# A residual block with three-pass matmuls: late gate sigmoids, an output-weight load split between gate loads, and two broadcast rows on another queue

## The chip, the cores and the metric

The kernel runs on one core of a Trainium2 chip. The metric is the device time of one execution in microseconds (us). The time before is the median of three runs. One more execution was profiled; every duration below comes from that one.

## What is computed

One layer of a streaming encoder: 1024 tokens, width 1024, all in float32. The parts that matter here:

```
proj = h @ w_in                       # q, k, v, forget logits, g_b, g_c, hc, gate_conv, gate_attn
ya = g_b * conv3(g_c * hc)            # branch a, 512 wide
yb = softmax(q k / 8 + c_q - c_k) v   # branch b, 8 heads of 64; c = running sum of log-sigmoids
m  = sigmoid(gate_conv) * (ya @ w_branch[0]) + sigmoid(gate_attn) * (yb @ w_branch[1])
x  = x + rmsnorm(m @ w_out)
x  = x + rmsnorm(swiglu(rmsnorm(x)))
```

The order in which sums are formed is free; the gates, the two branch products and the sum `m` are what the change works on.

## The kernel before, in words

**Arithmetic.** Each float32 matmul is done as three float32r passes: an operand is split into a high half (ScalarE copies it, `split`, line 132) and a low half (VectorE subtracts), and `mm3` (line 137) issues high-high, high-low and low-high. On top of that the large products use a Strassen-like scheme: seven block products whose names (A11, A12, A22, S1 to S4 for the weight side, B11, B21, B22, T1 to T4 for the other) appear all over the code. The trace puts every instruction on line 77, since a wrapper records them, so groups are told apart by tile names.

**Stages.** Projection (`strassen` per pair of weight columns, `jobs` 0 to 18, loop index `ij`), the last of these beside the first steps of attention (`last_pair`, line 915), attention with branch a's products filled in (`pba`), then branch b, then `w_out` (tiles `p`, `q`, `b`), the norms, the feed-forward part.

**Order.** In most stages a scheduler may reorder an engine's instructions; `strict[0]` names the engines on which program order is kept. In branch b it is SyncE and TensorE first, then VectorE and ScalarE too (lines 1546 to 1596). SyncE issues almost all loads, GpSimd most stores. Each of them waits in order: a DMA whose buffer isn't free holds back everything that stands behind it on that queue.

**Branch b.** The products of w_branch[1] and yb come in three groups. The first products A11 and S1 fill eight PSUM banks, `pbanks` and `vbanks` (`pbp`, `pbv` in the trace). The first loop over u = 0 to 3 (line 1569) does S2 into `pbanks[u]`, S4 into `vbanks[u]`, S3 into `pbanks[u]`, 18 matmuls a turn. Between S2 and S3 ScalarE copies `pbanks[u]` to `u_s[u]` (tile `temps`), and S3 can't start before that copy. VectorE adds, then `merge` (line 1513) multiplies by a gate and adds the result into `um`. The second loop (line 1588) does A22 and A12, 12 matmuls a turn, with its own merges. After it `first` (line 1650) starts `w_out` with operands that `first_ops` (line 1462) splits from `um`, and `sums` forms the others.

**Gates.** Blocks 0 to 6 of gate_attn lie in DRAM (`sg_dram`) as sigmoids. Block 7 lies there raw, since its projection runs beside attention. `gate` (line 1496) loads a 256 KB half block and, for block 7, issues its sigmoid on ScalarE at once. Half n1 of blocks 0 to 3 is loaded ahead of the first loop into the four buffers of `sg`; blocks 4 to 7 reuse these as merges free them (`early`). For half n2, blocks 7, 6, 1 and 0 go into buffers `raw` and `sx`, the other four into `sg` again (`late`).

**w_out's first block.** `load_wo(B11, u)` on line 1562 loads the four quarters of tile `x0`, 512 KB each, from `wo_dram`, within the loop of S1.

**Attention's first rows.** `cb_of(j, e)` (line 746) broadcasts the row of c for one head to 128 partitions (tile `cb`, two buffers, 512 KB). The two buffers are at first `bh` and `bl`, from which `wb_load` (line 994) stores the split w_branch to `wb_dram` on GpSimd's queue, the last time in job 13. The first two rows are asked for in job 15 (line 1081). They are first used by `mask_of(0, 7)` in `last_pair`.

Of the kernel before, what the change touches and what calls it, by code (L numbers as in the profile page):

```python
# [12 lines left out]
AF = mybir.ActivationFunctionType  # L13
# [4 lines left out]
P = 128  # L18
S = 1024
D = 1024  # L20
KT = D // P
# [21 lines left out]
B11, B21, B22, T1, T2, T3, T4 = range(7)  # L43
# [4 lines left out]
def block_kernel(  # L48
# [20 lines left out]
    class InOrder:  # L69
# [15 lines left out]
    nc = SimpleNamespace(  # L85
        **{e: InOrder(e) for e in engines}
    )
# [28 lines left out]
    def mul(o, a, b):  # L116
        nc.vector.tensor_tensor(o, a, b, op=ALU.mult)
# [32 lines left out]
    c_dram = dpool.tile([H, S], F32, name="c_dram")  # L150
# [21 lines left out]
    ones = cpool.tile([P, P], F32, name="ones")  # L172
    nc.vector.memset(ones, 1.0)
    mask = cpool.tile([P, P], F32, name="mask")
    def bcast_row(row, p, **kw):
        g = p.tile([P, row.shape[-1]], F32, **kw)
        nc.sync.dma_start(g, row.partition_broadcast(P))
        return g

    def st_tile(name, w=1):  # L180
# [363 lines left out]
    def raw_t():  # L544
        return wtile("raw", 3)

    def hi_t():
        return wtile("hi", 4, F32R)

    def lo_t():  # L550
        return wtile("lo", 3, F32R)

    def s4_t():
        return wtile("s4", 1, F32, (P, 4, P))

    def s4h_t():
        return wtile("s4h", 2, F32R, (P, 4, P))

    def s4l_t():
        return wtile("s4l", 2, F32R, (P, 4, P))  # L560
# [129 lines left out]
    def wcols(c0):  # L690
        return win[:, c0 : c0 + P]
# [54 lines left out]
    def cb_of(j, e, again=False):  # L746

        key = j, e, again
        if key not in cbs:
            p = t1 if j % 2 and not again else t0_  # L750
            cbs[key] = bcast_row(c_dram[2 * j + e], p, tag="cb", name="cb", bufs=2)
        return cbs[key]

    cbs, qks, stacks, vs_, rsums = {}, {}, {}, {}, {}
# [288 lines left out]
    for ij, (kind, j, _, _) in enumerate(jobs):  # L1043
        work = side.pop(ij, [])

        def mid():
            for cut, _ in work:
                pinned(cut, "vector", "scalar")

        if ij == 2:  # L1050
            logf_pre = forget_sums()
        if ij == 4:
            cs_ = forget_store(*logf_pre)
        if ij == 5:
            forget_turn(cs_)
        if ij < 2:
            if ij == 0:
                r1 = raw_t()
                nc.sync.dma_start(r1, kmaj(wcols(jobs[1][2])))
                t0_.tile([P, S], F32, tag="p", name="room", bufs=2)  # L1060
                h1, l1 = (
                    kblk(t0_.tile([P, S], F32R, tag="cb", name=n, bufs=2)) for n in ("h1", "l1")
                )
                split(h1, l1, r1)
                heads = [prep_first(None, t) for t in ((r0, h0, l0), (r1, h1, l1))]
                for _ in range(2):
                    bank(psm, "spare")
                strict[0] = ("tensor", "scalar")
                firsts = strassen_firsts([w for w, _ in heads], h1b, psm, pp)
                strict[0] = ()  # L1070
            (w, r1), (c11, p1) = heads[ij], firsts[ij]
            w = {**w, **prep_rest(wcols(jobs[ij][3]), r1)}
            if ij == 1:
                pairs.q.append(pairs.prep(*pairs.srcs.popleft()))
            _, c12, c21, c22 = strassen(w, h1b, psm, pp, p1, mid)
        elif ij < len(jobs) - 1:
            if ij == 12:
                k_load(0)
                q_load(0)
            w = pairs.get()  # L1080
            if ij == 15:
                cb_of(0, 0)
                cb_of(0, 1)
            c11, c12, c21, c22 = strassen(w, h1b, psm, pp, None, mid)
        else:
            w = pairs.get()
            psm_close()
            strict[0] = engines
            pss, pss_close = pool("pss", space=PSUM)
            c11, c12, c21, c22 = last_pair(w)  # L1090
        if kind == "qk":
            so = pp.tile([P, NC], F32, tag="so", name="so")
            copy(so, c11)
            for r, c, t in ((0, n1, so), (0, n2, c12), (1, n1, c21), (1, n2, c22)):
                nc.gpsimd.dma_start(qk_dram[j][r, :, c], t)
        elif kind == "z":
            zt = z_tile("zt")
            mul(zt[:, n1], c21, c11)
            mul(zt[:, n2], c12, c22)
            zts[j] = zt  # L1100
        elif kind == "gb":
            for m, parts in ((j, (c11, c12)), (j + 1, (c21, c22))):
                zt = zts.pop(m)
                for n in range(2):
                    o = n * NC
                    ot = pp.tile([P, NC], F32, tag="so", name="ot")
                    nc.vector.tensor_scalar(
                        ot, zt[:, o : o + NC], cw[:, 2, m : m + 1], None, op0=ALU.mult
                    )
                    for t in (1, 0):  # L1110
                        back = 2 - t
                        skip = 0 if n else back
                        nc.vector.scalar_tensor_tensor(
                            ot[:, skip:], zt[:, o + skip - back : o + NC - back],
                            cw[:, t, m : m + 1], ot[:, skip:],
                            op0=ALU.mult, op1=ALU.add,
                        )
                    yt = ot if parts[n] is c11 else parts[n]
                    mul(yt, ot, parts[n])
                    nc.gpsimd.dma_start(ya_dram[m][:, o : o + NC], yt)  # L1120
        else:
            so = c11
            strict[0] = ()
            if ij < len(jobs) - 1:
                so = pp.tile([P, NC], F32, tag="so", name="so")
                nc.scalar.activation(so, c11, AF.Sigmoid)
                for t in (c12, c21, c22):
                    nc.scalar.activation(t, t, AF.Sigmoid)
            for r, c, t in ((0, n1, so), (0, n2, c12), (1, n1, c21), (1, n2, c22)):
                nc.gpsimd.dma_start(sg_dram[j][r, :, c], t)  # L1130
        for _, store in work:
            pinned(store, "scalar")
        if ij < len(jobs) - 2:
            side[ij + 1].append(wo_load(ij))
        if ij + 1 in WB_AT:
            side[ij + 1].append(wb_load(WB_AT.index(ij + 1)))
# [314 lines left out]
    def load_wo(o, k):  # L1451
        nc.sync.dma_start(f32(wo[o][:, :, k, :]), wo_dram[o, k])
# [9 lines left out]
    def first_ops(i, th, tl):  # L1462
        a = slice(2 * i * P, (2 * i + 1) * P)
        if i:
            split(th, tl, um[:, :, a])
            firsts[i] = dict(A11=(th[:, LO], tl[:, LO]), A12=(th[:, UP], tl[:, UP]))
        else:
            firsts[i] = {}
            for o, src, h, l in zip(("A11", "A12"), blocks(i), th, tl):
                split(h, l, src)  # L1470
                firsts[i][o] = h, l
# [8 lines left out]
    def sums(i, t):  # L1480

        a11, a12, a21, a22 = blocks(i)
        s3[i] = t
        minus(i, t, a11, a21)
        minus(i, a21, a21, a22, ALU.add)
        minus(i, a11, a21, a11)
        minus(i, a12, a12, a11)
# [8 lines left out]
    def gate(d, ns, sg=None):  # L1496
        sg = sg_tile() if sg is None else sg
        nc.sync.dma_start(sg, sg_dram[d][1, :, ns])
        if d == KT - 1:
            nc.scalar.activation(sg, sg, AF.Sigmoid)  # L1500
        return sg

    def prod_b(ps, o, u, b, first):
# [7 lines left out]
            )  # L1511

    def merge(d, ns, t, c, sg):
        mul(t, c, sg)
        add(um[:, d, ns], um[:, d, ns], t)

# [42 lines left out]
    for u in range(4):  # L1559
        prod_b(vbanks[u], S1, u, T1, True)  # L1560
        copy(v_s[u], vbanks[u])
        load_wo(B11, u)
    load_wbr(A22)
    late = [
        x for t in (wtile("raw", 3), wtile("sx", 1)) for x in kept_halves(flat(t))
# [3 lines left out]
    for u in range(4):  # L1569
# [9 lines left out]
        merge(2 * u + 1, n1, v_s[u], v_s[u], sg1)  # L1579
        if u < 2:  # L1580
            early += [gate(2 * u + 4 + x, n1) for x in range(2)]
    first_ops(0, [s4h_t(), s4h_t()], [s4l_t(), s4l_t()])
    sums(0, s4_t())
    first_ops(1, hi_t(), lo_t())
    late |= {u: [gate(2 * u + 1 - x, n2) for x in range(2)] for u in (1, 2)}
    for u in range(4):
        load_wo(B21, u)
    for u in range(4):
        prod_b(pbanks[u], A22, u, T4, False)
        copy(v_s[u], pbanks[u])  # L1590
        prod_b(vbanks[u], A12, u, B21, False)
        copy(u_s[u], vbanks[u])
        for x, t in enumerate((v_s[u], u_s[u])):
            sg = late[u][x]
            merge(2 * u + 1 - x, n2, sg, t, sg)
    strict[0] = ("sync",)
    for n, o in ((3, T1), (2, T2)):
        wo[o] = x_tile(n)
# [306 lines left out]
    for f in range(NF):  # L1905
# [15 lines left out]
        for g, u, ns in ((g1, u1_, n1), (g2, u2, n2)):  # L1921
            sg = sgs[:, ns]
# [160 lines left out]
    sums = {n: wide(f"sum_{n}") for n in ("c11", "c12", "c22", "c21", "both", "rest", "neg")}  # L2083
# [107 lines left out]
```

## Time and profile before

| | |
|---|---|
| median of three runs (range) | 1333.67 us (1333.49 to 1334.63) |
| the profiled execution | 1333.1 us |
| its span, first to last instruction | 1331.3 us |
| mean granted TensorE clock | 0.993 |
| TensorE busy | 1305.8 us, 98% of the span |
| VectorE, ScalarE, GpSimd busy | 984.7, 572.4, 153.9 us |
| HBM traffic | 176 GB/s over the span |

TensorE is busy nearly always, so what matters is where it is not, and where its clock is down. The list of waits says for whom an engine waited, in total, how often and how long at most. The timeline gives start, duration, engine, operation, and in brackets the idle time before an instruction with what ended it. Matmuls of 512 columns overlap: they are 0.39 us each but start closer together.

### The profile page before, as it was taken

The numbers are of one execution on the slowest core, as the hardware profiler recorded it, in microseconds if no ns is written. First come the engines' busy times: TensorE is split into PE (matmuls) and PEld (weight loads), VectorE is DVE, ScalarE is ACT, GpSimd is POOL, SyncE is SP. The second block draws the span as 40 slices with busy tenths as digits, with TensorE's granted clock in tenths as the row PEclk, the third lists the DMA queues.
The fourth block names the chain that finished last, engine by engine and source line by source line (L and its number), as shares of the span: only waits on it lengthen the run. The fifth ranks groups of instructions, "written<-read, shape, count | busy, mean of one in ns | idle before, by whom it ended". The sixth has DMA issues, their size and how long they took to land.

```text
span 1331.3 us, 18049 instructions
## 1 busy us (share of the span) xinstructions
PE 1305.8 (98%) x6686; PEld 1087.1 (82%) x6686; DVE 984.7 (74%) x1525; ACT 572.4 (43%) x910; POOL 153.9 (12%) x287
## 2 busy tenths in 40 slices
PE   9999999999999999959999999999999999999997
PEld 8988888888787888848888888888888888888886
DVE  6975978876566867639699688997767776676685
ACT  6642432244345866515577432322322233443452
POOL 0011100021112221001012112121011101000000
PEclk9999999999999999979999999999999999999999
DMA  6337755677855444558466555563233328875541
GB/s 221 114 113 219 211 156 144 185 242 205 226 154 179 159 144 159 197 190 311 179 221 200 180 165 183 168 195 103 73 119 103 119 91 285 316 257 190 158 166 64
DMA packets 207240, 235.13 MB, mean 177 GB/s; under 512 B 12064, under 2 KB 150368, under 8 KB 207152
## 3 DMA queue, kind: packets, MB, share of 16 engines
q1 hardware_dynamic: 159424, 157.13, 37.7%
q0 software_dynamic: 18544, 62.17, 12.7%
q10 hardware_dynamic: 29184, 14.68, 4.4%
q8 instruction: 52, 0.85, 0.3%
q14 instruction: 36, 0.29, 0.1%
HBM read 161.79 MB, written 72.16 MB: 176 GB/s over the span
## 4 chain that ended last, share of the span: by engine, by line
PE 73%; issue 17%; DMA 3%; POOL 2%; DVE 2%; ACT 1%; SPq 0%; DVEq 0%; POOLq 0%; ACTq 0%
PE b L77 36%; PE pd L77 16%; PE pba L77 3%; PE pv L77 3%; PE tps L77 3%; PE po L77 3%; PE p L77 2%; PE sp L77 2%; PE pbp L77 2%; PE ma L77 1%; DMA raw<-sg_dram 1%; PE q L77 1%; PE tp L77 1%; POOL wb_dram L77 1%; DMA wb_dram<-bl 1%
## 5 line engine op out<-in xcount | busy, mean ns | idle before, releaser
L77 PE MATMUL b<-x,hi 128*128 128x512 f32 x1088 | 335.4, 389 | 0.0
L77 PEld LDWEIGHTS b<-x,hi 128*128 128x128 f32 x1088 | 204.1, 188 | 42.4
L77 PE MATMUL b<-x,lo 128*128 128x512 f32 x544 | 211.7, 389 | 0.0
L77 DVE TENSOR_TENSOR c<-c,b 128x512 f32<-128x512 f32 x193 | 131.5, 682 | 47.0 <-PE b L77 38.6
L77 DVE TENSOR_TENSOR lo<-raw,hi 128x1024 fp32r<-128x1024 f32 x90 | 108.4, 1204 | 71.2 <-PE b L77 61.1
L77 ACT ACTIVATE hi<-raw 128x1024 fp32r<-128x1024 f32 (+1 forms) x96 | 97.4, 1017 | 94.0 <-PE b L77 46.7
L77 PEld LDWEIGHTS b<-x,lo 128*128 128x128 f32 x544 | 102.1, 188 | 21.2
L77 ACT ACTIVATE hi<-sx 128x1024 fp32r<-128x1024 f32 (+1 forms) x42 | 43.8, 1043 | 136.8 <-PE b L77 128.8
L77 ACT ACTIVATE sgf<-c 128x512 f32<-128x512 f32 x31 | 19.6, 633 | 131.9 <-DVE c L77 112.8
L77 DVE TENSOR_TENSOR lo<-sx,hi 128x1024 fp32r<-128x1024 f32 (+1 forms) x42 | 50.3, 1198 | 28.8 <-PE b L77 26.1
L77 DVE TENSOR_TENSOR sx<-raw 128x512 f32<-128x512 f32 x78 | 53.6, 687 | 19.7 <-DMA raw<-in_w_in_dram 10.7
L77 PE MATMUL pd<-hi,lo 128*128 128x512 f32 x160 | 62.3, 389 | 0.0
L77 PE MATMUL pd<-hi 128*128 128x512 f32 x160 | 61.9, 390 | 0.0
L77 PE MATMUL pd<-ghi 128*128 128x512 f32 x148 | 57.7, 390 | 0.0
L77 PE MATMUL pd<-glo,ghi 128*128 128x512 f32 x148 | 57.6, 389 | 0.0
L77 PE MATMUL pd<-ghi,glo 128*128 128x512 f32 x148 | 57.6, 389 | 0.0
L77 PE MATMUL b<-hT12h,lo 128*128 128x512 f32 x136 | 53.0, 390 | 0.0
L77 PE MATMUL b<-hT12h,hi 128*128 128x512 f32 x136 | 52.9, 389 | 0.0
L77 PE MATMUL b<-hT34h,lo 128*128 128x512 f32 x136 | 52.9, 389 | 0.0
L77 PE MATMUL b<-hT34h,hi 128*128 128x512 f32 x136 | 52.9, 389 | 0.0
L77 PE MATMUL b<-hT34l,hi 128*128 128x512 f32 x136 | 52.9, 389 | 0.0
L77 PE MATMUL b<-hT12l,hi 128*128 128x512 f32 x136 | 52.9, 389 | 0.0
(462 smaller groups left out, 3065.1 us busy)
## 6 DMA issues: line engine op xcount, KB each, us to landing
raw<-in_w_gate_up_dram SPq DMA_DIRECT2D x55, 512.0 KB, 3.9
raw<-in_w_in_dram SPq DMA_DIRECT2D x35, 512.0 KB, 5.9
x<-wo_dram SPq DMA_DIRECT2D x28, 512.0 KB, 7.8
a_dramS<-um POOLq DMA_DIRECT2D x44, 256.0 KB, 3.0
a_dramA<-um POOLq DMA_DIRECT2D x33, 256.0 KB, 2.7
wo_dram<-h ACTq DMA_DIRECT2D x16, 448.0 KB, 4.3
wo_dram<-l ACTq DMA_DIRECT2D x16, 448.0 KB, 4.8
sg<-sg_dram SPq DMA_DIRECT2D x28, 256.0 KB, 2.7
```

The source lines that it names most:

```text
L77: ins = getattr(self.engine, name)(*args, **kw)
```

## The change

Three edits. First, the sigmoid of a gate of block 7 moves from `gate` (at the load) into `merge` (at the use). Second, the four loads of `x0` leave the loop of S1 and go in pairs behind the gate loads of the first two turns of the first loop, and the block `first_ops(0)`, `sums(0)`, `first_ops(1)` moves from between the two loops to behind the first turn of the second one. Third, the first two broadcast rows are issued on GpSimd's queue, and in job 14 instead of 15; later rows stay on SyncE.

```diff
-    def bcast_row(row, p, **kw):
+    def bcast_row(row, p, by=None, **kw):
         g = p.tile([P, row.shape[-1]], F32, **kw)
-        nc.sync.dma_start(g, row.partition_broadcast(P))
+        (by or nc.sync).dma_start(g, row.partition_broadcast(P))
...
-            cbs[key] = bcast_row(c_dram[2 * j + e], p, tag="cb", name="cb", bufs=2)
+            by = nc.sync if j else nc.gpsimd
+            cbs[key] = bcast_row(c_dram[2 * j + e], p, by, tag="cb", name="cb", bufs=2)
...
-            if ij == 15:
+            if ij == 14:
                 cb_of(0, 0)
                 cb_of(0, 1)
...
         nc.sync.dma_start(sg, sg_dram[d][1, :, ns])
-        if d == KT - 1:
-            nc.scalar.activation(sg, sg, AF.Sigmoid)
         return sg
...
     def merge(d, ns, t, c, sg):
+        if d == KT - 1:
+            nc.scalar.activation(sg, sg, AF.Sigmoid)
         mul(t, c, sg)
...
         copy(v_s[u], vbanks[u])
-        load_wo(B11, u)
...
             early += [gate(2 * u + 4 + x, n1) for x in range(2)]
-    first_ops(0, [s4h_t(), s4h_t()], [s4l_t(), s4l_t()])
-    sums(0, s4_t())
-    first_ops(1, hi_t(), lo_t())
+            for k in range(2):
+                load_wo(B11, 2 * u + k)
...
             merge(2 * u + 1 - x, n2, sg, t, sg)
+        if u == 0:
+            first_ops(0, [s4h_t(), s4h_t()], [s4l_t(), s4l_t()])
+            sums(0, s4_t())
+            first_ops(1, hi_t(), lo_t())
```

The place on ScalarE where the sigmoids stood, before: `raw_5813` is block 7's half n2, `sg_5878` its half n1; `temps<-pbp` are the copies between S2 and S3.

```order
L77 ACTIVATE temps_5652<-pbv_5776 128x512
L77 ACTIVATE raw_5813<-raw_5813 128x512
L77 ACTIVATE temps_5652<-pbp_5709 128x512
L77 ACTIVATE pbv_5773<-p_s_5653 128x512
L77 ACTIVATE temps_5652<-pbp_5710 128x512
L77 ACTIVATE pbv_5774<-p_s_5653 128x512
L77 ACTIVATE sg_5878<-sg_5878 128x512
L77 ACTIVATE temps_5652<-pbp_5711 128x512
L77 ACTIVATE pbv_5775<-p_s_5654 128x512
```

The same engine now, from the third turn of the first loop on (`sg_5875` is the same half n1, the last `temps<-pbp_5709` belongs to the second loop):

```order
L77 ACTIVATE temps_5652<-pbp_5711 128x512
L77 ACTIVATE pbv_5775<-p_s_5654 128x512
L77 ACTIVATE temps_5652<-pbp_5712 128x512
L77 ACTIVATE pbv_5776<-p_s_5654 128x512
L77 ACTIVATE sg_5875<-sg_5875 128x512
L77 ACTIVATE temps_5652<-pbp_5709 128x512
L77 ACTIVATE temps_5652<-pbv_5773 128x512
L77 ACTIVATE s4h_5962<-um_3816 128x512
```

No sigmoid stands ahead of a copy of the first loop any more: half n1's follows the last of them, and half n2's the last copy of the second loop. The split of `um` for `first_ops(0)` (`s4h`) now follows the second loop's first two copies.

SyncE's loads in branch b, as the difference (`raw<-wb_dram` are A12's weights, the `hi` and `wbl` behind them A22's; then gates):

```order
 L77 DMA lo<-wb_dram 128x1024
 L77 DMA raw<-wb_dram 128x1024 x2
-L77 DMA x_5650<-wo_dram 128x2x512 x4
 L77 DMA hi<-wb_dram 128x1024
 L77 DMA wbl<-wb_dram 128x1024
...
 L77 DMA sg<-sg_dram_138 128x512
 L77 DMA sg<-sg_dram_139 128x512
+L77 DMA x_5650<-wo_dram 128x2x512 x2
 L77 DMA sg<-sg_dram_140 128x512
 L77 DMA sg<-sg_dram_141 128x512
+L77 DMA x_5650<-wo_dram 128x2x512 x2
```

The 2 MB of `x0` no longer stand ahead of A22's weights and the gates of blocks 7, 6, 1 and 0; they stand behind the gates of blocks 4 and 5, and 6 and 7.

GpSimd's queue around job 14, as the difference (`sg_dram_137` and `sg_dram_138` are stores of jobs' gates):

```order
 L77 DMA sg_dram_137<-c_3088 128x512
 L77 DMA wb_dram<-bl 128x2x512
+L77 DMA cb<-c_dram 128x1024
 L77 DMA sg_dram_137<-c_3072 128x512
+L77 DMA cb<-c_dram 128x1024
 L77 DMA sg_dram_138<-so 128x512
```

The two rows now stand behind the stores that free their buffers and ahead of two gate stores. On SyncE they stood between two weight loads (`raw<-in_w_in_dram`) of one job, which now follow each other.

## The prediction

> **What bounds the kernel now.** I read the page first. TensorE is busy for nearly the whole span, so a gain must come out of its gaps:
>
> ```profile
> PE 1305.8 (98%) x6686; PEld 1087.1 (82%) x6686; DVE 984.7 (74%) x1525; ACT 572.4 (43%) x910; POOL 153.9 (12%) x287
> ```
>
> Then TensorE's list of waits, of which two rows lie where the change works:
>
> ```profile
> PE pbp L77 <- ACT temps L77: 14.5, 2, 11.0
> ...
> PE b L77 <- ACT c L77: 0.7, 1, 0.7
> ```
>
> The first row is branch b's first loop, the second a gate job of the projection. TensorE's timeline shows where the long waits lie, and where the loops begin and end (564.30 is the first S2, 599.38 the first A22, 610.26 w_out's first matmul):
>
> ```profile
> 564.30 0.39 PE L77 MATMUL pbp<-yh,hi 128*128 128x512 f32 x1
> ...
> 566.80 0.39 PE L77 MATMUL pbv<-yh,lo 128*128 128x512 f32 x1
> 578.21 0.80 PE L77 MATMUL pbp<-yh,hi 128*128 128x512 f32 x1 [11.02 <-ACT temps L77]
> ...
> 592.20 0.50 PE L77 MATMUL pbp<-yh,hi 128*128 128x512 f32 x1 [3.44 <-ACT temps L77]
> ...
> 599.38 0.39 PE L77 MATMUL pbp<-yh,hi 128*128 128x512 f32 x1
> ...
> 610.26 0.62 PE L77 MATMUL p<-x,s4h 128*128 128x512 f32 x2
> ```
>
> ScalarE's timeline shows that the copies were not slow. They stood, in program order, behind a sigmoid whose gate had not landed:
>
> ```profile
> 577.04 0.63 ACT L77 ACTIVATE raw<-raw 128x512 f32<-128x512 f32 x1 [11.94 <-DMA raw<-sg_dram]
> 577.57 0.58 ACT L77 ACTIVATE temps<-pbp 128x512 f32<-128x512 f32 x1
> ...
> 591.03 0.63 ACT L77 ACTIVATE sg<-sg 128x512 f32<-128x512 f32 x1 [4.93 <-DMA sg<-sg_dram]
> 591.57 0.58 ACT L77 ACTIVATE temps<-pbp 128x512 f32<-128x512 f32 x1
> ```
>
> The waits cost clock too. Right after the long one the windows view gives a granted clock of 0.58 (third column from the end):
>
> ```profile
> 576.00:584.00 8.00, 5.79 (x16) 4.65 (x17) 4.14 (x6) 2.32 (x4) 0.00 (x0) 0.58 0.33 116
> ```
>
> **Branch b, first loop.** The second loop is undisturbed: 48 matmuls from 599.38 to 610.26, 10.88 us, 0.2267 us each. At that pace the 72 matmuls of the first loop take 16.32 us; they took 599.38 - 564.30 = 35.08. The excess is 18.76 us: waits of 11.02 and 3.44, and 4.30 of slow clock. If no sigmoid stands before a copy, the first copy can run when S2 ends, about 565.9, takes 0.58, and is done before S4 ends at 567.2. So the wait goes and S3 follows S4. Nothing is added: the two sigmoids, 0.63 each, go where ScalarE is idle most of the time.
>
> What is late next? The weights first. S3's low half is the later one, and A22's stands behind `x0`:
>
> ```profile
> 559.24 0.38 SPq L77 DMA_DIRECT2D lo<-wb_dram  x1
> ...
> 560.68 3.15 SPq L77 DMA_DIRECT2D x<-wo_dram  x4
> ...
> 564.65 0.43 SPq L77 DMA_DIRECT2D wbl<-wb_dram  x1
> 566.08 1.55 SPq L77 DMA_DIRECT2D raw<-sg_dram  x2
> ```
>
> The issue views give their times to landing, 4.3 us for S3's, 11.7 for A22's, 10.9 for the gates behind it; 2.7 for the eight gates that come after the rush, and 7.8 as the page's median for `x0` and its like:
>
> ```profile
> lo<-wb_dram SPq DMA_DIRECT2D x1, 512.0 KB, 4.3
> ```
> ```profile
> wbl<-wb_dram SPq DMA_DIRECT2D x1, 512.0 KB, 11.7
> ```
> ```profile
> raw<-sg_dram SPq DMA_DIRECT2D x2, 256.0 KB, 10.9
> ```
> ```profile
> sg<-sg_dram SPq DMA_DIRECT2D x8, 256.0 KB, 2.7
> ```
> ```profile
> x<-wo_dram SPq DMA_DIRECT2D x28, 512.0 KB, 7.8
> ```
>
> S3's weights are there at 563.5, in time for 567.2. The second loop would begin at 564.30 + 16.32 = 580.6 and w_out at 591.5. A22's weights landed at 564.65 + 11.7 = 576.4 even behind `x0`; without its 2 MB ahead they come sooner. The gates for half n2 landed at 577, also in time. The gate of block 4 can be loaded when the first merge has read its buffer (about 568.7) and is wanted at the third turn, 564.30 + 3 x 4.08 - 1.36 + 0.7 = 575.9 (4.08 being 18 matmuls, 1.36 six, 0.7 the add ahead): 7 us for a load of 2.7. Block 7's buffer comes free near 575, and its sigmoid is wanted near 581.5: 6 us. `x0`'s second pair goes out near 575.5 and lands by 583.3, against 591.5. So the moved loads cost nothing, with some 3 us to spare at the tightest gate.
>
> VectorE is the next limit. Its timeline shows six operations a turn, then the stretch from the first split to the last merge, back to back; below it, the one GpSimd operation that ran while VectorE was idle:
>
> ```profile
> 584.78 0.69 DVE L77 TENSOR_TENSOR temps<-temps,pbv 128x512 f32<-128x512 f32 x1 [1.47 <-PE pbv L77]
> ...
> 588.27 0.69 DVE L77 TENSOR_TENSOR um<-um,temps 128x512 f32<-128x512 f32 x1
> ...
> 602.40 2.39 DVE L77 TENSOR_TENSOR s4l<-um,s4h 128x512 fp32r<-128x512 f32 x2
> ...
> 606.95 1.77 DVE L77 TENSOR_TENSOR sx<-temps,sx 128x512 f32<-128x512 f32 x1
> 608.76 0.69 DVE L77 TENSOR_TENSOR um<-um,sx 128x512 f32<-128x512 f32 x1
> ...
> 618.54 0.68 DVE L77 TENSOR_TENSOR um<-um,raw 128x512 f32<-128x512 f32 x1
> ```
> ```profile
> 589.11 1.25 POOL L77 TENSOR_TENSOR s<-um 128x512 f32<-128x512 f32 x1 [23.37 <-DVE um L77]
> ```
>
> A turn is 588.96 - 584.78 = 4.18 us, against TensorE's 4.08. From 567.3 four turns end at 584.0. The stretch behind them, 602.40 to 619.22, is 16.8; its operations are only put in another order (the first turn's merges now come ahead of the splits), so the last merge ends near 600.8, 9.3 us after w_out's first matmul; before, 619.22 - 610.26 = 9.0. W_out's third `first` needs those merges, and comes 24 matmuls of `first` and 24 of `second`, 10.9 us, after its start, with a ScalarE copy and a VectorE subtraction still between. So that place has nothing to spare now, and 0.3 us of lateness there are TensorE's. The GpSimd operation of 1.25 us will run beside a busy VectorE; beside GpSimd a VectorE operation took 1.77 us for 0.69, so it may cost up to 1.1. I charge 0.5 for both, between ends of 0 and 1.4. The first splits of `first_ops`, moved behind four merges (some 2.7 us), end near 590, the second near 592; they are wanted at 592 and 594.7, so the move is covered by the second loop's 10.88 us. Branch b gives 18.76 - 0.5 = 18.3 us.
>
> **The broadcast rows.** ScalarE's copies `so<-b` come once a gate job; the pitch is 19.04 us, but 20.08 around this place, a loss of 1.04:
>
> ```profile
> 342.56 0.58 ACT L77 ACTIVATE so<-b 128x512 f32<-128x512 f32 x1
> ...
> 362.64 0.58 ACT L77 ACTIVATE so<-b 128x512 f32<-128x512 f32 x1
> ...
> 381.68 0.57 ACT L77 ACTIVATE so<-b 128x512 f32<-128x512 f32 x1
> ```
>
> The cause is on SyncE: it waited for the store of `bh` before the first row, and the weight load behind the rows went out late; VectorE waited 4.31 us for it. First the row of SyncE's waits, then its timeline, then VectorE's:
>
> ```profile
> SPq L77 <- DMA wb_dram<-bh: 4.7, 1, 4.7
> ```
> ```profile
> 343.87 0.38 SPq L77 DMA_DIRECT2D raw<-in_w_in_dram  x1
> ```
> ```profile
> 341.82 1.22 DVE L77 TENSOR_TENSOR lo<-raw,hi 128x1024 fp32r<-128x1024 f32 x1 [2.03 <-PE b L77]
> ...
> 350.94 0.69 DVE L77 TENSOR_TENSOR sx<-raw 128x512 f32<-128x512 f32 x1 [4.31 <-DMA raw<-in_w_in_dram]
> ```
>
> Off SyncE's queue, the load can go when its buffer is read, 343.04, 0.8 us sooner, and not in line behind 1 MB of rows. That should cover the 1.04. GpSimd takes the same wait instead, and holds two gate stores behind it; their tiles are wanted a job later, 19 us, so this is free. Ends: 0 and 1.04; I take 1.0, since the delay was made by the queue.
>
> The Trainium skill speaks against this part: by "DMA: Bandwidth & Descriptors", section "Issuing engines are not separate DMA queues", DMAs run on the same 16 engines whoever issues them, and another issuer saves only the sequencer's time. By it this part gives nothing, and the time would be 1.0 us longer; the row of 4.7 us, a sequencer that waits, speaks for a gain.
>
> **The sum.** 18.3 + 1.0 = 19.3 us. The profiled execution took 1333.1 us (span 1331.3), so it would take 1313.8. The median of the runs is 1333.67, 0.6 above it; on it the sum gives 1314.4. The stages behind are TensorE's too and start from the same lags, so nothing is given back there.
>
> **The rivals.**
> 1. The rows' transfers fill the DMA engines as before, and the weight load lands no sooner: 1314.4 + 1.0 = 1315.4.
> 2. A wait stays in branch b: the gates of blocks 4 to 7 land late. At 10.9 us instead of 2.7 block 4's lands at 579.8, wanted at 575.9; VectorE is 4 us late and, with nothing to spare at w_out's third product, so is TensorE: 1318.4. For it: SyncE's loads are many here. Against: 2 MB of `x0` no longer stand ahead of them. If the wait also costs clock, half of 4.30 comes on top, 1320.5. The Trainium skill's "TensorE: Matmul & The Clock Gate", section "What's actually happening", halves the clock after an idle window of about 3.4 us; by it only a wait of that length or more pays this.
> 3. The change doesn't remove the wait: S3 waited for something that landed with the gate. Then only the rows' 1.0 is left, 1332.7. Against: S3's weights landed at 563.5.
> 4. Slower: the broadcast from GpSimd's queue is slow, and attention waits. GpSimd first uses the rows at 387.18, and on SyncE's queue one landed in 6.0 us:
>
> ```profile
> 387.18 1.75 POOL L77 TENSOR_TENSOR cb<-cb,mask 128x128 f32<-128x128 f32 x2
> ```
> ```profile
> DMA to landing us min/median/max: 6.0/6.0/6.0
> ```
>
> From an issue near 343.6 a row has 43.6 us; each us beyond costs one, and the gain is used up at 43.6 + 19.3 = 62.9 us, ten times the row: at 67 us, 1337.8. Nothing in the trace points there.
>
> **How the numbers follow.** Forecast 0.72, rival 1 0.10, rival 2 0.15, rival 3 0.02, rival 4 0.01. The time is the forecast's, 1314.4. Low end: with no charge on VectorE and all 1.04 of the rows, 19.8 us, 1313.9; less 1.1, the width of the runs (1333.49 to 1334.63), 1312.8. High end: the first three cases up to a wait of 4 us, 1318.4. A measurement of this kernel tells about 0.2% (2.7 us) from no change: forecast and rivals 1 and 2 are faster, 0.97; rival 3 is within, 0.02; rival 4 slower, 0.01.
>
> **What would show it.** Right: TensorE's list has no row `pbp <- ACT temps`; A22 starts 16.3 us after the first S2, w_out 27.2 us after it; the clock is 1.00 between; `so<-b` keeps 19.04 throughout. Wrong: a wait of `pbp`, or of w_out's `p`, of over 2 us; ScalarE waiting for `sg` before a `temps<-pbp`; or a gap in attention's first steps.

## The result, and the profile after

The changed kernel takes 1315.15 us, the median of four runs (1314.85 to 1315.42), against 1333.58 (1333.27 to 1334.63) for four runs of the kernel before. The ratio is 0.986, its 95% interval 0.9843 to 0.9877. That is 18.4 us faster, and 0.75 us above the forecast of 1314.4.

The page of the changed kernel has TensorE busy for 99% of the span:

```profile
PE 1301.5 (99%) x6686; PEld 1084.5 (83%) x6686; DVE 984.6 (75%) x1525; ACT 572.3 (44%) x910; POOL 154.9 (12%) x289
```

From its list of TensorE's waits (total, times, longest), in which no wait is over 1.5 us:

```profile
PE tp L77 <- DVE hn L77: 0.6, 2, 0.4
PE b L77 <- ACT c L77: 0.6, 1, 0.6
PE p L77 <- DVE lo L77: 0.5, 1, 0.5
```

The row `pbp <- ACT temps` of 14.5 us is gone. The row `b <- ACT c`, which belongs to the place of the broadcast rows, is still there, 0.6 instead of 0.7. The row of `p` is new, and the row `tp <- DVE hn` was 0.2 before. TensorE's timeline has the marks of branch b (first S2, first A22, w_out's first matmul) and the new wait:

```profile
564.58 0.39 PE L77 MATMUL pbp<-yh,hi 128*128 128x512 f32 x1
...
580.90 0.39 PE L77 MATMUL pbp<-yh,hi 128*128 128x512 f32 x1
...
591.78 0.39 PE L77 MATMUL p<-x,s4h 128*128 128x512 f32 x1
...
603.82 0.50 PE L77 MATMUL p<-x,lo 128*128 128x512 f32 x1 [0.53 <-DVE lo L77]
```

The first loop takes 580.90 - 564.58 = 16.32 us, and w_out starts 27.20 after the first S2; before, it was 610.26 - 564.30 = 45.96. The difference is 18.76, the figure of the prediction to the last digit. The windows view gives TensorE busy for all of this stretch, at a clock of 1.00 (third column from the end):

```profile
564.58:591.78 27.20, 27.20 (x121) 22.53 (x120) 23.52 (x31) 11.91 (x20) 5.99 (x5) 1.00 0.93 332
```

ScalarE's timeline shows the copy between S2 and S3 waiting only for TensorE, and the two sigmoids waiting for nothing:

```profile
566.14 0.60 ACT L77 ACTIVATE temps<-pbp 128x512 f32<-128x512 f32 x1 [0.76 <-PE pbp L77]
...
581.80 0.62 ACT L77 ACTIVATE sg<-sg 128x512 f32<-128x512 f32 x1
...
592.48 0.62 ACT L77 ACTIVATE raw<-raw 128x512 f32<-128x512 f32 x1
```

The spans close the account: 1331.3 - 1313.6 = 17.7 us less. Branch b gives 18.76. From w_out's first matmul to the end it is 1313.6 - 591.78 = 721.82 us, before 1331.3 - 610.26 = 721.04: 0.78 given back. And the first S2 comes at 564.58 instead of 564.30, 0.28 later. 18.76 - 0.78 - 0.28 = 17.70. So in the profiled executions what lies ahead of branch b, the place of the broadcast rows included, has won nothing. ScalarE's copies `so<-b` show that place in the changed kernel:

```profile
342.89 0.58 ACT L77 ACTIVATE so<-b 128x512 f32<-128x512 f32 x1
362.79 0.58 ACT L77 ACTIVATE so<-b 128x512 f32<-128x512 f32 x1
381.82 0.58 ACT L77 ACTIVATE so<-b 128x512 f32<-128x512 f32 x1
```

The pitch is 19.90 at the place and 19.03 behind it: 0.86 over 19.04 is lost, where 1.04 was lost before.

### The profile page after: what moved, and what is told of

It is laid out like the page before. It is cut to its first block, busy times and chain, and to the rows that moved or that the text cites. A ratio compares the mean times of both kernels' runs of the same rounds, so it can differ in the third digit from the quotient of the medians.

```text
span 1313.6 us, 18050 instructions
## 1 busy us (share of the span) xinstructions
PE 1301.5 (99%) x6686; PEld 1084.5 (83%) x6686; DVE 984.6 (75%) x1525; ACT 572.3 (44%) x910; POOL 154.9 (12%) x289
## 4 chain that ended last, share of the span: by engine, by line
PE 92%; DVE 3%; DMA 2%; ACT 1%; issue 1%; SPq 0%; DVEq 0%; ACTq 0%
PE b L77 57%; PE pd L77 16%; PE pba L77 3%; PE pv L77 3%; PE tps L77 3%; PE po L77 3%; PE p L77 2%; PE sp L77 2%; DVE temps L77 1%; PE ma L77 1%; PE tp L77 1%; PE mb L77 1%; DMA raw<-in_w_gate_up_dram 1%; DMA raw<-in_w_in_dram 1%; DMA xt<-in_x_dram 1%
## 5 line engine op out<-in xcount | busy, mean ns | idle before, releaser
L77 POOL DMA_DIRECT2D a_dramA<-um x33 | 17.9, 541 | 299.6 <-DVE um L77 298.9
```

Of the source, the lines that this page charges most:

```text
L77: ins = getattr(self.engine, name)(*args, **kw)
```

## The experiments

There were two questions. What in branch b made the gain: the sigmoid's place, the loads, or both? And why did the rows give next to nothing? For the first, my theory was that the sigmoid standing ahead of the copies was the whole stall, with the load order deciding only what is late next; the rival was that late loads made it. For the second, the theory of the prediction was SyncE's queue, the rival was DMA engines that are full whoever issues. Four kernels start from the kernel before, four from the changed one. The first four were measured beside runs of the kernel before with a median of 1333.92 us, the last four beside runs with 1333.34. Three kernels ran once; for them only the trace is read, since one time can't rank kernels that lie this close.

### The sigmoid alone

```diff
         nc.sync.dma_start(sg, sg_dram[d][1, :, ns])
-        if d == KT - 1:
-            nc.scalar.activation(sg, sg, AF.Sigmoid)
...
     def merge(d, ns, t, c, sg):
+        if d == KT - 1:
+            nc.scalar.activation(sg, sg, AF.Sigmoid)
```

> The kernel before with the first edit alone: block 7's sigmoids in merge. Theory (the place of the sigmoids on ScalarE is what held TensorE; the moved loads only keep the gates in time): no wait of pbp on ScalarE's copies, but block 4's gate lands near 578 to 580 behind x0 and is wanted near 576, so VectorE is 3 to 4 us late, and so is TensorE at w_out's third product (rival 2's price): 1317 to 1320 us. Rival (the gates are in time even behind x0, the move of x0 is worth nothing): 1315.0 to 1316.0. Rival (the move of the loads is what counts): over 1324, with a wait of pbp of over 5 us left.

Measured: 1321.12 us (1320.34 to 1322.68), ratio 0.9906 [0.9891, 0.9921]. The wait of S3 is gone, and w_out starts 593.13 - 565.93 = 27.20 us after the first S2, as in the changed kernel. But VectorE's timeline has a gate that is late, TensorE's a wait at w_out's third product, and the windows view a clock that falls behind it:

```profile
581.33 0.69 DVE L77 TENSOR_TENSOR temps<-temps,sg 128x512 f32<-128x512 f32 x1 [3.52 <-DMA sg<-sg_dram]
```
```profile
606.86 0.93 PE L77 MATMUL p<-x,hi 128*128 128x512 f32 x2 [2.69 <-ACT hi L77]
608.12 0.80 PE L77 MATMUL p<-x,lo 128*128 128x512 f32 x1 [0.33 <-DVE lo L77]
608.71 1.05 PE L77 MATMUL p<-x,hi 128*128 128x512 f32 x2
...
610.99 0.62 PE L77 MATMUL p<-x,hi 128*128 128x512 f32 x2
```
```profile
603.00:607.00 4.00, 1.31 (x7) 0.77 (x6) 3.41 (x7) 1.25 (x2) 0.00 (x0) 1.00 0.73 269
607.00:610.00 3.00, 2.67 (x7) 1.66 (x8) 3.00 (x4) 3.00 (x6) 0.00 (x0) 0.54 1.03 343
```

VectorE is 3.52 us late, and TensorE pays 2.69 + 0.33 of it. From 606.86 to 610.99 stand three groups of three matmuls, 4.13 us, where later groups are 0.68 apart: 4.13 - 2.04 - 0.33 = 1.76 us is slow clock. From w_out's start to the end this kernel takes 1318.9 - 593.13 = 725.77 us, 3.95 more than the changed one. So it is the sigmoid that made the stall, and the order of the loads decides whether the gates come in time without it. How `x0` made the gate late stands in SyncE's timeline:

```profile
574.36 4.04 SPq L77 DMA_DIRECT2D sg<-sg_dram  x4
```

VectorE had read the buffer of this gate (block 4's) by 570.33, but the load went out 4.03 us later; in the changed kernel it went out at once (569.02, read by 568.99). In between SyncE waited twice for loads of `x0` to land, 3.8 us in all by its list of waits. So most of the lateness was made in SyncE's queue, ahead of the gate's own transfer. The time lies 1.1 us above the highest that I had expected; in this trace 2.18 us are lost at the broadcast rows, 1.14 more than in that of the kernel before.

### The loads alone

The gates' sigmoids stay at the load; `x0` and `first_ops` move as in the change.

```diff
         copy(v_s[u], vbanks[u])
-        load_wo(B11, u)
...
             early += [gate(2 * u + 4 + x, n1) for x in range(2)]
+            for k in range(2):
+                load_wo(B11, 2 * u + k)
```

> The kernel before with the second edit alone: x0 in pairs behind the gates, first_ops and sums behind the second loop's first turn, the sigmoids still at the loads. Theory (the sigmoids' place holds TensorE): ScalarE still waits for block 7's half n2, which lands near 572 instead of 577, and for half n1 later; two waits of pbp remain, the first near 5.5 us; 1326 to 1330 us. Rival (the loads count): 1315 to 1319.

Measured: 1328.75 us (1328.03 to 1330.44), ratio 0.9962 [0.995, 0.9975], within the range expected. ScalarE's timeline and TensorE's show the old chain, shortened:

```profile
572.16 0.63 ACT L77 ACTIVATE raw<-raw 128x512 f32<-128x512 f32 x1 [6.72 <-DMA raw<-sg_dram]
...
585.96 0.63 ACT L77 ACTIVATE sg<-sg 128x512 f32<-128x512 f32 x1 [4.88 <-DMA sg<-sg_dram]
```
```profile
573.33 0.79 PE L77 MATMUL pbp<-yh,hi 128*128 128x512 f32 x1 [5.81 <-ACT temps L77]
587.13 0.50 PE L77 MATMUL pbp<-yh,hi 128*128 128x512 f32 x1 [3.39 <-ACT temps L77]
605.20 0.62 PE L77 MATMUL p<-x,s4h 128*128 128x512 f32 x2
```

From the first S2 at 564.64 to w_out it is 40.56 us, 13.36 over the undisturbed 27.20. The waits are 5.81 and 3.39, and the other 4.16 is clock. Without `x0` ahead the gate lands sooner, so the first wait falls from 11.02 to 5.81; the second is about the same. The loads alone are worth 5.2 us, the sigmoid alone 12.8, and the rival, that late loads made the stall, would have needed all 18.

### The sigmoid and x0, without moving first_ops

The kernel before with the sigmoid in `merge` and `x0` moved; `first_ops`, `sums` and the rows stay where they were.

> The kernel before with the sigmoids in merge and x0 moved, first_ops and sums still between the two loops, rows as before. Theory (moving first_ops is free either way, since the splits are wanted 10 us later, and VectorE's work up to the last merge is the same): 1315.0 to 1316.0, the same wait of about 0.5 us at w_out's third product. Rival (ScalarE's copies of the second loop, queued behind splits that wait for the first loop's last merge, hold TensorE): 1317 or more, with a wait of pbp, pbv or p of over 1.5 us.

Measured: 1315.75 us (1315.28 to 1316.56), ratio 0.9865 [0.985, 0.988]. W_out starts 592.70 - 565.50 = 27.20 us after the first S2, and the wait at its third product is that of the changed kernel:

```profile
604.86 0.50 PE L77 MATMUL p<-x,lo 128*128 128x512 f32 x1 [0.52 <-DVE lo L77]
```

So moving `first_ops` is worth nothing either way. Of the 1.1 us between the spans of the two traces, 0.63 is the broadcast rows' place again, 1.49 lost here against 0.86.

### Half of x0 ahead of the gates

The changed kernel, with the first two quarters of `x0` back in the loop of S1, ahead of A22's weights and the gates:

```diff
         copy(v_s[u], vbanks[u])
+        if u < 2:
+            load_wo(B11, u)
...
-            for k in range(2):
-                load_wo(B11, 2 * u + k)
+            if u:
+                for k in range(2):
+                    load_wo(B11, 2 * u + k)
```

> The changed kernel with the first pair of x0's loads back ahead of A22's weights and the gates, 1 MB instead of the 2 MB of the run with the sigmoids alone. Theory (each MB ahead delays block 4's gate by 2.6 us, and VectorE's lateness reaches w_out's third product one for one): VectorE waits about 0.9 us for a gate (3.5 there), w_out's third product about 1.4 us in all (3.0 there); the clock holds if a wait must reach about 3.4 us to lower it, as the Trainium skill has it, and is down for some 10 matmuls if a shorter wait is enough, as the 2.7 us wait there suggests. 1316 to 1317.5 us. Rival (the gates are late only when all 2 MB stand ahead): as the changed kernel, 1315.2.

Measured in one execution: 1315.66 us, 0.3 below the range I had expected. VectorE's timeline and TensorE's:

```profile
577.38 0.69 DVE L77 TENSOR_TENSOR temps<-temps,sg 128x512 f32<-128x512 f32 x1 [1.73 <-DMA sg<-sg_dram]
```
```profile
602.78 0.73 PE L77 MATMUL p<-x,hi 128*128 128x512 f32 x2 [0.76 <-ACT hi L77]
604.04 0.50 PE L77 MATMUL p<-x,lo 128*128 128x512 f32 x1 [0.53 <-DVE lo L77]
```

The gate is 1.73 us late, half of 3.52, and TensorE waits 1.29 us in all, 0.76 more than in the changed kernel. From w_out's start to the end it is 722.92 us, 1.10 more. The wait for gates is twice the 0.9 that I had expected, that of w_out's third product near the 1.4. That is rival 2 of the prediction in small: 2 MB ahead make the gates 3.5 us late, 1 MB 1.7, none leaves them in time.

### The rows alone

The kernel before with the third edit only (GpSimd's queue, asked for in job 14).

> The kernel before with the third edit alone: the rows on GpSimd's queue in job 14. Theory (the DMA engines, not SyncE's queue, make the weight load late): pitch of so<-b 19.9 us at this place, wait of b 0.6, as in the full change; about 1333.3 us. Rival (the queue is the cause and something else in the full change hid it): pitch 19.1, 1332.6.

Measured in one execution: 1335.29 us; span 1333.5. The copies `so<-b`, and VectorE waiting for the weight load behind the rows:

```profile
342.77 0.57 ACT L77 ACTIVATE so<-b 128x512 f32<-128x512 f32 x1
363.95 0.57 ACT L77 ACTIVATE so<-b 128x512 f32<-128x512 f32 x1
```
```profile
352.25 0.69 DVE L77 TENSOR_TENSOR sx<-raw 128x512 f32<-128x512 f32 x1 [5.41 <-DMA raw<-in_w_in_dram]
```

The pitch is 21.18, so 2.14 is lost with the rows off SyncE's queue, more than on it. The theory of the queue wanted 19.1; as the whole cause it falls. That the loss was larger than 0.86 neither theory had. Over the traces it was 1.04, 0.85, 1.49 and 2.18 with the rows on SyncE (before and the three kernels above that keep them there), and 0.86, 2.14 and 0.28 with the rows on GpSimd (after, this one, half of x0). The two ranges overlap; what goes with the loss on each side stands in the table below, in the part on the rows.

### The rows a job later

If the engines are full, the 1 MB must move in time, not between queues. In the kernel before the rows were asked for in job 15 and the first was issued at 340.17; in the changed one they were asked for in job 14 and it was issued at 340.75. Both times it went out after a wait for the store of `bh`, so asking a job earlier had moved nothing. `pinned` keeps program order for one call on the queue that it names.

```diff
-            if ij == 14:
-                cb_of(0, 0)
-                cb_of(0, 1)
+            if ij == 16:
+                for e in range(2):
+                    pinned(lambda: cb_of(0, e), "gpsimd")
```

> The changed kernel with the two rows issued on GpSimd's queue a job later still, behind the rush of stores and weight loads, held there by program order. Theory (the DMA engines are full at this place, and the rows' 1 MB makes the weight load late, whoever issues it): the pitch of so<-b falls from 19.9 to 19.1 or less, the weight load lands in under 6 us, the wait of b for ScalarE's c is gone; 1314.2 to 1314.6 us. Rival (the stores of wb_dram and wo_dram alone fill the engines): pitch 19.9, as before.

Measured: 1314.01 us (1313.83 to 1314.6), ratio 0.9851 [0.983, 0.9872]. GpSimd issues the rows at 367.1 and 371.2 now. In order: the copies `so<-b`, VectorE, the weight load's issue with its time to landing, and the windows view (DMA share in the last column but one):

```profile
342.61 0.58 ACT L77 ACTIVATE so<-b 128x512 f32<-128x512 f32 x1
361.65 0.57 ACT L77 ACTIVATE so<-b 128x512 f32<-128x512 f32 x1
380.69 0.57 ACT L77 ACTIVATE so<-b 128x512 f32<-128x512 f32 x1
```
```profile
347.62 0.69 DVE L77 TENSOR_TENSOR sx<-raw 128x512 f32<-128x512 f32 x1 [0.93 <-DMA raw<-in_w_in_dram]
```
```profile
raw<-in_w_in_dram SPq DMA_DIRECT2D x1, 512.0 KB, 4.3
```
```profile
344.00:348.00 4.00, 4.00 (x19) 3.32 (x18) 2.41 (x4) 1.70 (x2) 0.58 (x2) 1.00 0.77 203
```

The pitch is 19.04 throughout and TensorE waits for nothing at this place. The load lands in 4.3 us and the engines' share is 0.77. The trace shows 0.86 us less lost than in the changed kernel. The medians differ by 1.1 us, but they were taken beside different runs of the kernel before, and the two intervals overlap, so the times alone do not rank these two.

### The same on SyncE's queue

The kernel above with `by = nc.sync` and `pinned(..., "sync")`: later, but on the queue of the kernel before.

> The same place for the two rows, a job later, but on SyncE's queue, behind both weight loads of the job. Theory (when the rows move, not who issues them, decides): pitch 19.1 or less in the job where 19.9 stood, like the run with GpSimd's queue. Rival (SyncE's queue itself makes loads late): a pitch over 19.4 in this job or the next, or a wait of b of over 0.5 us.

Measured in one execution: 1314.7 us. SyncE issues both rows at 363.19, and the pitch is 19.04 as well:

```profile
342.61 0.58 ACT L77 ACTIVATE so<-b 128x512 f32<-128x512 f32 x1
361.65 0.58 ACT L77 ACTIVATE so<-b 128x512 f32<-128x512 f32 x1
```

When the rows are loaded decides here, and not who loads them.

### Splits in halves

This aims at the 0.53 us left at w_out's third product: the rows a job later, and `first_ops` splits the lower half of a block ahead of the upper one, so that the first `lo` is done sooner.

```diff
         if i:
-            split(th, tl, um[:, :, a])
+            for half in (LO, UP):
+                split(th[:, half], tl[:, half], um[:, half, a])
```

> The run with the rows a job later on GpSimd's queue, and first_ops of pairs 1 to 3 splitting the two halves of a block one after the other, so that w_out's third product waits for a half block on ScalarE and VectorE. Theory (that place waits for VectorE's chain, with nothing to spare): the wait of p for VectorE's lo, 0.5 us, is gone; 1313.7 to 1314.1. Rival (the merges themselves end too late): a wait of 0.3 or more stays.

Measured: 1315.23 us (1314.46 to 1316.2), ratio 0.9859 [0.9841, 0.9878], outside the range expected and no faster than without the halves. TensorE's list has no wait of `p` any more, but a new one, and the wait for `hn` is as in the changed kernel (0.2 with the rows a job later and whole splits):

```profile
PE b L77 <- DMA x<-wo_dram: 0.6, 2, 0.4
PE tp L77 <- DVE hn L77: 0.6, 2, 0.3
```

From w_out's start to the end it is 1313.1 - 591.08 = 722.02 us, against 1312.2 - 590.48 = 721.72 with whole splits. The wait was removed and the time given back behind it, where these two rows together are 1.0 us more. Of the 0.9 us between the spans, 0.6 lies ahead of w_out, where the two kernels are the same. Whether the halves caused these or they vary by run, as they do between other kernels here, stays open.

## Why the prediction was right, and where it was off

**Branch b, first loop: right.** The excess of 35.08 over 16.32 us was the stall and its clock, and it went as a whole: 18.76. The two kernels with one edit each show that neither edit is enough alone: the sigmoid's place removes the wait, and the loads keep the gates in time once it is removed. Moving `first_ops` was rightly costed at nothing.

**What is late next: the place was right, the slack was not.** I had the gate of block 4 landing 2.7 us after its issue with over 4 us to spare, and some 3 us at the tightest gate, block 7's. SyncE's timeline, the landing time of that load, and VectorE's first use of it:

```profile
569.02 2.37 SPq L77 DMA_DIRECT2D sg<-sg_dram  x2
```
```profile
DMA to landing us min/median/max: 6.2/6.2/6.2
```
```profile
576.50 1.35 DVE L77 TENSOR_TENSOR temps<-temps,sg 128x512 f32<-128x512 f32 x1
...
600.73 0.68 DVE L77 TENSOR_TENSOR um<-um,raw 128x512 f32<-128x512 f32 x1
602.54 2.36 DVE L77 TENSOR_TENSOR lo<-um,hi 128x1024 fp32r<-128x1024 f32 x2 [1.13 <-ACT hi L77]
```

It landed near 575.2 and was used at 576.50: 1.3 us to spare. The 2.7 came from gates loaded while the DMA engines' share was between 0.20 and 0.33; here it is 0.93. Rival 2 was therefore nearer than the text made it, and the kernel with half of `x0` ahead of the gates crosses over.

**VectorE: right, charged 0.5.** The one VectorE operation that now ran beside GpSimd's took 1.35 us instead of 0.69. The last merge ends at 601.41, 9.63 us after w_out's start, where 9.3 was forecast and 9.0 stood before; TensorE waits 0.53 at exactly the place named. All of the stretch from w_out's start to the end gave back 0.78. That includes 0.4 more of waiting for `hn` in a later stage, which was not forecast.

**The rows: the failing step.** The prediction took 1.0 us "since the delay was made by the queue". The measured gain is 0.18 in the pitch, and the kernel with this edit alone lost more than the one before. SyncE's wait was indeed taken over by GpSimd, as these rows show for its first row in the changed kernel. And the weight load was issued earlier by as much as forecast. Its job runs 0.33 us later in this trace (`so<-b` at 342.89 instead of 342.56), so it is counted from there: 0.55 us behind the copy instead of 1.31, 0.76 sooner. But it took longer, 7.0 us before and 7.5 after, so that VectorE starts 8.20 us behind the copy instead of 8.38: only 0.18 of the 0.76 arrives.

```profile
340.75 0.57 POOL L77 DMA_DIRECT2D cb<-c_dram  x1 [5.20 <-DMA wb_dram<-bh]
```
```profile
raw<-in_w_in_dram SPq DMA_DIRECT2D x1, 512.0 KB, 7.0
```
```profile
raw<-in_w_in_dram SPq DMA_DIRECT2D x1, 512.0 KB, 7.5
```
```profile
351.09 0.69 DVE L77 TENSOR_TENSOR sx<-raw 128x512 f32<-128x512 f32 x1 [4.13 <-DMA raw<-in_w_in_dram]
```

The same figures from every trace, in us ("issue" is how long behind `so<-b` the weight load goes out, "lost" the pitch less 19.04):

| kernel | rows by | issue | landing | VectorE's wait | lost |
|---|---|---|---|---|---|
| loads alone | SyncE | 1.21 | 6.9 | 4.13 | 0.85 |
| before | SyncE | 1.31 | 7.0 | 4.31 | 1.04 |
| sigmoid and x0 | SyncE | 2.12 | 6.6 | 4.77 | 1.49 |
| sigmoid alone | SyncE | 2.65 | 6.7 | 5.45 | 2.18 |
| half of x0 | GpSimd | 0.55 | 7.0 | 3.55 | 0.28 |
| after | GpSimd | 0.55 | 7.5 | 4.13 | 0.86 |
| rows alone | GpSimd | 0.55 | 8.8 | 5.41 | 2.14 |
| rows later | GpSimd | 0.55 | 4.3 | 0.93 | 0.00 |
| rows later | SyncE | 0.55 | not in the view | 0.83 | 0.00 |
| rows later, halves | GpSimd | 0.55 | 5.8 | 2.43 | 0.00 |

Where anything is lost, the loss is VectorE's wait less 3.27 or 3.28 us: that much lateness is free here. With the rows at their old place on SyncE the landing hardly changes and the loss follows the issue, so the queue does set it there, as the prediction had it. (In the kernel with the sigmoid alone the store of `bh`, for which the first row waits, left 1.48 us later than before.) With the rows on GpSimd the issue is always the earliest, and the loss follows the landing, which varies. Taking the rows off SyncE's queue thus ends one delay and leaves the load with another.

A reason can be read in the windows view, first of the kernel before, then of the changed one:

```profile
344.00:348.00 4.00, 4.00 (x20) 3.30 (x19) 2.02 (x3) 1.69 (x2) 0.59 (x2) 1.00 0.91 245
```
```profile
344.00:348.00 4.00, 4.00 (x19) 3.34 (x18) 2.02 (x3) 1.70 (x2) 1.00 (x3) 1.00 0.96 311
```

The DMA engines' share is 0.91 and 0.96 while the load is under way; with the 1 MB gone it is 0.77 and the load lands in 4.3. The share alone does not rank the kernels, though: with the rows later and the halves it is 0.88 and nothing is lost, in the kernel with the sigmoid and `x0` 0.87 and 1.49 is lost. That the 1 MB beside the load is what costs is shown by the two kernels that move it; that it does so by filling the engines is argued from the share. So a sequencer that waited 4.7 us was real, and yet removing its wait gained little. This is rival 1, and the rule of the Trainium skill that stood behind it, "DMA: Bandwidth & Descriptors", section "Issuing engines are not separate DMA queues", holds: another issuer won 0.76 us of the sequencer's time, and 0.18 of it was left at the landing. I should have read the DMA share of this place beside the wait, and given the rule more than a tenth.

**The sum.** 18.3 + 1.0 was forecast. 18.76 - 0.78 = 17.98 came from branch b and behind, and 0.18 from the rows, which other small differences ahead of branch b took back: with the 0.28 us at the first S2 it is 17.7 in the profiled execution. Between the medians it is 18.4. That the forecast lies only 0.75 us off is in part luck: the profiled execution was forecast at 1313.8 us and took 1315.41, 1.6 more, and the median of 1315.15 is nearer to rival 1's 1315.4 than to the forecast.

## What to carry to other kernels

On an engine that works in order, look what stands ahead of a copy that TensorE waits for: work that itself waits for a DMA belongs at its use, and the transfers must then be put in the order in which they become due. Before moving a transfer to another queue, read the DMA share while the late transfer is under way; if it is near 0.9 or above, as here, move bytes in time and not between issuers, and see in the trace that they really moved. How long a transfer takes to land is to be taken from rows where the DMA engines are as busy as at its new place (6.2 us here, not 2.7).

## What the runs showed of the hardware beyond that

**The clock falls after shorter waits than I allowed for.** A wait of 2.69 us was followed by a granted clock of 0.54 and cost 1.76 us of slow matmuls. The Trainium skill's "TensorE: Matmul & The Clock Gate", section "What's actually happening", gives an idle window of about 3.4 us; the measurement decides, and 2.69 was enough here. In that trace the clock was still 1.00 from 605 to 607 us and fell just after the matmuls had resumed at 606.86 (0.61 over the next us, then 0.50). After the waits of 0.76 and 0.53, close to one another in the kernel with half of `x0`, the windows view shows 1.00:

```profile
602.78:606.00 3.22, 2.69 (x11) 1.92 (x12) 3.22 (x4) 1.94 (x3) 0.00 (x0) 1.00 0.99 329
```

After a wait of 0.94 us at 356.85, in the kernel with the sigmoid alone, it shows 1.00 as well. Where between 0.94 and 2.69 the fall begins no run shows. The price grows little with the wait. From the end of a wait to the next mark, less the matmuls between at 0.2267 us each, the slow clock cost 2.39 us after 11.02 and 1.74 after 3.44 (before), 2.25 after 5.81 and 1.75 after 3.39 (the loads alone), beside the 1.76 after 2.69.

**A crowded stretch makes a load's landing vary.** With the rows on GpSimd and the load issued 0.55 us behind the copy each time, it took 7.0, 7.5 and 8.8 us to land, and the loss was 0.28, 0.86 and 2.14. Why it differs no run shows. One execution of such a place can't rank two kernels.
